# A one-core hybrid Hyena/S5 block: transfers issued earlier, x normalized in halves, the gate sums in 16 double steps, and one full-precision copy moved from VectorE to ScalarE

## The chip, the cores and the metric

One core of a Trainium2 chip, one launch of one program. The metric is device time in microseconds (us), first to last instruction of the core and what lies around it. TensorE (PE) multiplies, VectorE (DVE), ScalarE (ACT) and GpSimd (POOL) do the elementwise work, SyncE (SP) issues nearly all of the transfers, and each engine takes its instructions strictly in program order.

## The reference, cut to what matters

```
cond = silu(c), silu(c_ctx);  mod = cond @ w_ada + b_ada          # six parts of 1024: shift, scale, gate, twice
pc = (rms_norm(ctx) * g * (1 + scale_c) + shift_c) @ w_in         # 256 context tokens, S5 channels only
ctx_state = final S5 states of pc                                 # both directions
px = (rms_norm(x) * g * (1 + scale_x) + shift_x) @ w_in           # 1024 tokens: 1536 Hyena channels, 512 S5
yh = x0 * (fft_long_conv(x1 * v, filter) + bias * x1 * v)         # x0, x1, v: px after a 3-tap convolution
ys = gelu(S5 scan of px, started from ctx_state, both directions)
ys = ys * sigmoid(ys @ w_glu + b_glu)
x  = x + mod[2] * rms_norm(concat(yh, ys) @ w_out)
hx = modulated_norm(x, mod[3], mod[4])
x  = x + mod[5] * rms_norm(ConvGLU(hx))                           # w_up, 3x3 depthwise convolution, w_down
```

Everything is float32.

## The kernel before

A float32 matrix product is done as three matmuls on rounded operands: every operand is a rounded "high" tile (fp32r, made by ACT with a copy) and a "low" tile (what is left after subtraction of the high one, made by DVE or POOL), and lines 228, 229 and 230 issue high x high, low x high and high x low. So each piece of data passes through ACT and then DVE (or POOL) before PE can take it. Helpers record the engines' work, so one line stands for many places: line 143 is a two-tensor operation (`tt`), 146 a tensor-scalar one (`ts`), 149 a fused one (`stt`), 152 a load or store on SP's queue (`ld`), 161 an activation (`act`).

A scheduler decides the order of each engine's list from the program order and estimated due times. POOL's list is kept as written throughout, those of DVE and ACT from line 641 to 828, and SP's from line 1031 on. PE's list is always reordered. Buffers come from pools, so a transfer into a reused buffer waits until the last reader of its former content is done.

The stages, by the profile's clock: 
- 0 to 51 us, the front. Blocks of `w_ada` (512 KB each) are multiplied with the two condition vectors (line 308), giving shift and scale. x comes in as four tiles of 128 x 2 x 1024; for each, `sums_sq` (ACT, Square with a row sum into PSUM) gives the squares. `norm(c, n)` makes n columns of 1/rms (ACT square root, a few DVE operations of 128 x 8), and `apply` scales x (DVE, two operations of 128 x 1024 per tile). The modulation row is turned by four transposes (line 592), x by line 648, in eight column blocks, and `x_cols` (ACT from PSUM, with scale and shift per partition, then a DVE subtraction) makes the high and low operands.
- 51 to 120 us, the first projection (`x_mm`, eight steps), with the filter's work beside it. Ahead of the loop stands a scaling by -1 of `Cc[1]`, a table loaded as `k_c`.
- 120 to 205 us, the context: `ctx_cols` transposes a column block of ctx into PSUM (line 717), then makes c2's high part (ACT, Identity with scale and shift, rounded), the full value cv (DVE, tensor-scalar, from the same PSUM), and the low part (DVE, cv minus high).
- 205 to 405 us, four groups of Hyena channels, eight S5 batches' matmuls, and between them `gate_sums`: 32 steps, eight for each of mod parts 3, 4, 2 and 5. A step loads a block of `w_ada`, 1024 x 128, as one transfer of 512 KB into the ring `wm` of one buffer (`macc` takes the copied result), multiplies (line 691, 16 matmuls of 128 columns with 32 rows of output: eight matmuls, each of two passes), copies the 128 x 128 result to `acc` (ACT), sums its four row groups with a matmul against `sel` (line 693), adds the bias (ACT, Identity) and loads the next block. `sums_next(i)` takes a step; `MS` and `M_WIN` say how many steps stand at which places of the S5 loop.
- 405 to 585 us, the rest of S5 and of the Hyena spectra (`u_spec`, `product`, `inverse`; the latter on PE is line 1078), and the GLU gate of S5: `glu_w` (load a half of w_glu, split it), `glu_y` (split the S5 output), `glu_high`, `glu_low` (lines 1187, 1195) and in `glu_low` the sigmoid (ACT, into a single buffer `sg`) and the product ysT[n] * sg (DVE, 128 x 1024).
- 585 to 1445 us, w_out, the ConvGLU up and down, and the output.

Of the kernel before, what the change touches and what calls it, by code (L numbers as in the profile page):

```python
# [108 lines left out]
def hybrid_block(ctx: ExitStack, tc: tile.TileContext, t, out):  # L109
# [19 lines left out]
    def FRing(n, *dims, at=None):  # L129
        return Ring(sa, n, *dims, at=at)  # L130
# [541 lines left out]
    def gate_sums(gates, wm, acc, b0):  # L672
# [4 lines left out]
        def load(n):  # L677
            if n < len(steps):
# [7 lines left out]
        for n, (i, h) in enumerate(steps):  # L686
            w = ws_.pop(n)
            w3_ = w.rearrange("p (k c) -> p k c", k=8)
            for k in range(8):
                j = k % 4  # L690
                PE.matmul(PS[32 * j:32 * j + 32, b0[0], 0:128], lhsT=cond[:, k], rhs=w3_[:, k], start=k < 4, stop=k >= 4)  # L691
# [22 lines left out]
    def ctx_cols(k):  # L714
# [6 lines left out]
        ts(V, cv.rearrange("p j c -> p c j"), q, A0[:, k, 1:2], B0[:, k, 1:2], MUL, ADD)  # L721
# [35 lines left out]
    sums = gate_sums((3, 4, 2, 5), wm, macc, gb)  # L757
# [39 lines left out]
    for k in range(8):  # L797
# [366 lines left out]
    graw, sg = F(2, 512, at=(7,)), F(1024, at=(7,))  # L1164
    xin = FRing(2, 1024, at=(7,))
# [416 lines left out]
```

## Time and profile before

| | us |
|---|---|
| median of 3 runs (range) | 1447.63 (1445.07 to 1448.21) |
| the profiled execution | 1447.4 |
| its span, first to last instruction | 1445.6 |
| PE busy | 1326.1 (92%) |
| DVE busy | 883.5 (61%) |
| ACT busy | 482.3 (33%) |
| POOL busy | 472.5 (33%) |
| mean granted TensorE clock | 0.951 |

The execution is that of the profile, 1.8 us more than its span. "Busy" counts overlapping work per engine; PEld, the loading of weights into PE, runs beside the matmuls. An engine's average says little here, since the stages differ: each one is read by itself in the rows below. In a timeline row the first number is the start (us from the span's start), the second the time until the group's end, `xN` the count of instructions in it, and the bracket the idle time ahead of it with what ended it.

### The profile page before, as it was taken

How to read it: one execution, taken by the hardware profiler on the slowest of the kernel's cores; microseconds unless marked ns; L12 is line 12 of the kernel's file. 1: busy time of each engine (PE TensorE's matmuls, PEld its weight loads, DVE VectorE, ACT ScalarE, POOL GpSimd, SP SyncE). 2: the span in 40 equal slices, each digit the busy share in tenths (PEclk: the TensorE clock that was granted, in tenths of full speed). 3: DMA queues.
4: the chain of work that ended last, by engine and by line, in shares of the span. 5: the costliest groups of instructions: out<-in, count | busy, mean ns of one | idle time of the engine just before them, and what ended most of it. 6: DMA issues, size and time to landing. Idle time of an engine off the chain costs nothing.

```text
span 1445.6 us, 16905 instructions
## 1 busy us (share of the span) xinstructions
PE 1326.1 (92%) x6668; PEld 1071.5 (74%) x6668; DVE 883.5 (61%) x1208; ACT 482.3 (33%) x802; POOL 472.5 (33%) x250
## 2 busy tenths in 40 slices
PE   4888789899989957899999999999999999999997
PEld 0666567677767855787778888888888888888886
DVE  7776842456677999647766755755756757115314
ACT  3632122444433413346633222222222233224321
POOL 0000726556589203210122222222222226443540
PEclk8799899989998887999999999999999999999999
DMA  9423143545533225213311111111111115335422
GB/s 376 143 96 102 66 94 93 163 138 154 156 94 109 74 83 209 73 58 114 124 44 44 49 54 44 46 57 44 45 57 44 44 58 171 107 101 176 132 73 88
DMA packets 149639, 144.48 MB, mean 100 GB/s; under 512 B 29860, under 2 KB 128696, under 8 KB 147128
## 3 DMA queue, kind: packets, MB, share of 16 engines
q1 hardware_dynamic: 135000, 124.67, 27.9%
q10 hardware_dynamic: 14560, 18.74, 3.7%
q8 instruction: 52, 0.85, 0.2%
q14 instruction: 27, 0.22, 0.1%
HBM read 123.98 MB, written 19.37 MB: 99 GB/s over the span
## 4 chain that ended last, share of the span: by engine, by line
PE 73%; DVE 16%; DMA 5%; ACT 3%; issue 2%; SPq 1%; ACTq 0%; DVEq 0%
PE PS L228 21%; PE PS L229 21%; PE PS L230 21%; DVE s L143 12%; ACT s L161 3%; DMA s<-in_w_ada_dram 2%; DVE s L149 1%; PE PS L691 1%; PE PS L972 1%; DVE s L1001 1%; PE PS L428 1%; DMA s<-in_x_dram 1%; PE PS L936 1%; PE PS L429 1%; PE PS L1078 1%
## 5 line engine op out<-in xcount | busy, mean ns | idle before, releaser
L228 PE MATMUL PS<-s,s 128*128 128x512 f32 x1320 | 527.6, 401 | 4.2 <-ACT s L161 3.9
L229 PE MATMUL PS<-s,s 128*128 128x512 f32 x1320 | 524.1, 397 | 0.0
L230 PE MATMUL PS<-s,s 128*128 128x512 f32 x1320 | 523.1, 397 | 0.1
L161 ACT ACTIVATE s<-s 128x512 fp32r<-128x512 f32 (+9 forms) x356 | 259.6, 748 | 641.0 <-PE PS L229 208.2
L143 POOL TENSOR_TENSOR s<-s,s 128x1024 fp32r<-128x1024 f32 x98 | 252.2, 2577 | 613.5 <-ACT s L161 593.5
L143 DVE TENSOR_TENSOR s<-s,s 128x512 fp32r<-128x512 f32 (+6 forms) x178 | 196.8, 1117 | 218.7 <-ACT s L161 210.4
L143 POOL TENSOR_TENSOR s<-s 128x512 f32<-128x512 f32 (+2 forms) x147 | 219.0, 1503 | 262.4 <-PE PS L445 145.7
L228 PEld LDWEIGHTS PS<-s,s 128*128 128x128 f32 x1320 | 258.2, 196 | 59.9 <-ACT s L161 6.4
L230 PEld LDWEIGHTS PS<-s,s 128*128 128x128 f32 x1320 | 258.0, 196 | 53.8 <-issue 2.7
L229 PEld LDWEIGHTS PS<-s,s 128*128 128x128 f32 x1320 | 258.8, 196 | 52.5 <-issue 2.6
L149 DVE SCALAR_TENSOR_TENSOR s<-s,s 128x1024 f32<-128x1024 f32 x140 | 218.0, 1557 | 102.5 <-ACT s L161 98.3
L143 DVE TENSOR_TENSOR s<-s 128x512 f32<-128x512 f32 (+11 forms) x403 | 187.0, 500 | 41.9 <-DMA s<-s 27.1
L161 ACT ACTIVATE s<-PS 128x512 f32<-128x512 f32 (+6 forms) x212 | 110.8, 538 | 227.1 <-PE PS L429 53.2
L149 DVE SCALAR_TENSOR_TENSOR s<-s 128x1024 f32<-128x1024 f32 (+5 forms) x136 | 107.6, 807 | 54.9 <-ACT s L161 52.5
L161 ACT ACTIVATE s<-PS,s 128x128 f32<-128x128 f32 (+5 forms) x161 | 101.9, 680 | 81.7 <-PE PS L230 18.5
L143 DVE TENSOR_TENSOR s<-PS,s 128x512 f32<-128x512 f32 (+3 forms) x81 | 52.4, 668 | 62.5 <-ACT s L161 24.4
L230 PE MATMUL PS<-s 128*128 128x512 f32 x136 | 53.7, 395 | 0.0
L228 PE MATMUL PS<-s 128*128 128x512 f32 x136 | 53.4, 395 | 0.0
L229 PE MATMUL PS<-s 128*128 128x512 f32 x136 | 53.4, 392 | 0.0
L149 DVE SCALAR_TENSOR_TENSOR s<-PS,s,s 128x1023 f32<-128x1023 f32 x24 | 30.6, 1278 | 26.4 <-ACT s L161 25.9
L1078 PE MATMUL PS<-s,s 128*128 128x256 f32 x128 | 31.2, 406 | 15.6 <-DMA s<-in_k_idft_dram 14.8
L1078 PEld LDWEIGHTS PS<-s,s 128*128 128x128 f32 x128 | 26.1, 205 | 20.2 <-DVE s L143 16.1
(89 smaller groups left out, 803.0 us busy)
## 6 DMA issues: line engine op xcount, KB each, us to landing
s<-in_ffn_w_up_dram SPq DMA_DIRECT2D x44, 512.0 KB
s<-in_ffn_w_down_dram SPq DMA_DIRECT2D x44, 512.0 KB
s<-in_w_ada_dram SPq DMA_DIRECT2D x32, 512.0 KB
s<-in_w_in_dram SPq DMA_DIRECT2D x20, 512.0 KB
s<-in_w_ada_dram SPq DMA_DIRECT2D x8, 1024.0 KB
s<-in_x_dram SPq DMA_DIRECT2D x4, 1024.0 KB
kf_d<-s ACTq DMA_DIRECT2D x4, 1024.0 KB
s<-kf_d SPq DMA_DIRECT2D x4, 1024.0 KB
```

Source lines behind the costliest of these rows:

```text
L143: return pin(e, e.tensor_tensor(o, a, b, op=op))
L149: return pin(e, e.scalar_tensor_tensor(o, a, s, b, op0=op0, op1=op1))
L161: return pin(A, A.activation(o, i, f, **k))
L228: PE.matmul(dst, lhsT=hi, rhs=mh, start=first, stop=False)
L229: PE.matmul(dst, lhsT=hi, rhs=ml, start=False, stop=False)
L230: PE.matmul(dst, lhsT=lo, rhs=mh, start=False, stop=last)
L428: PE.matmul(o, lhsT=dft[:, c, r], rhs=hkb[:, r, 0], start=True, stop=False)
L429: PE.matmul(o, lhsT=dft[:, 2 * c, r2], rhs=hkb[:, r2, 1], start=False, stop=True)
L691: PE.matmul(PS[32 * j:32 * j + 32, b0[0], 0:128], lhsT=cond[:, k], rhs=w3_[:, k], start=k < 4, stop=k >= 4)
L936: PE.matmul(pk_[:, g], lhsT=d["G"][:, z, g * 128:(g + 1) * 128], rhs=CC[z][:, g].rearrange("p d q -> p (d q)"), start=z == 0, stop=z == 1)
L972: PE.matmul(PS[h:h + 64, bk, i * 160:(i + 1) * 160], lhsT=d["GT"][:, z, g * 128 + h:g * 128 + h + 64], rhs=u, start=True, stop=True)
L1078: PE.matmul(bk[:, 256 * j:256 * j + 256], lhsT=zb[:, k, c], rhs=idft[:, 2 * h + j, i], start=i == 0, stop=i == 3)
```

## The change

Four parts.

1. The front. `norm` and `apply` run for each half of x (four columns of row sums, two tiles) as soon as that half's squares are there, rather than once for all eight columns at the end. The scaling of `Cc[1]` moves from ahead of the projection loop to its step k = 3.
2. The context. The full value cv is made by ACT from PSUM with a second Identity activation, behind the rounded one; the DVE tensor-scalar goes. The rest of `ctx_cols` is unchanged.
3. The gate sums. 32 single steps become 16 double ones: a step multiplies two blocks (m = 0, 1) into 256 columns of PSUM, copies 128 x 256 at once, and issues the loads of the next two blocks. Each block comes as two transfers of 256 KB into four tiles (two halves of `wm`, two tiles of `w2_`). The summing matmuls and the bias (now a DVE two-tensor operation on 128 x 2) of a step stand at the head of the next one (`finish`). `gate_end`'s row goes through its own tile `grow_`. The sums are created behind `s5_load(0)`; `MS` goes from (1, 2, 2, 1, 1) to (1, 1, 1, 0, 1), and `sums_next(M_WIN)` leaves the context loop (M_WIN is 0).
4. The GLU gate. The raw w_glu has two buffers of its own at the top of a segment, and its two loads, `kf_load(3)`, `wo_load(4)`, `wo_load(5)` and the inverse DFT table in two halves are issued ahead of the load of ys4; before, ys4 came first, then the table, the two halves of w_glu in turn through one buffer, the w_out blocks, and the spectrum.

```diff
@@ the loop over w_ada blocks, and what follows it
-    norm(2, 8)
-    for q in range(4):
-        apply(V, xr[q], 2 + 2 * q)
+            if (k - SQ0) % 2:
+                h = k - SQ0 - 1
+                norm(2 + 2 * h, 4)
+                for q in (h, h + 1):
+                    apply(V, xr[q], 2 + 2 * q)
@@ gate_sums
-                ld(ws_[n].rearrange("p (k c) -> p k c", k=8),
-                   w_ada[:, c0:c0 + 128].rearrange("(k p) c -> p k c", p=128))
+                for u in range(2):
+                    ld(ws_[n][u].rearrange("p (k c) -> p k c", k=4),
+                       w_ada[512 * u:512 * u + 512, c0:c0 + 128].rearrange("(k p) c -> p k c", p=128))
...
-            act(acc, PS[:, b0[0], 0:128], AF.Copy)
-            PE.matmul(PS[:, b0[0], 128:130], lhsT=acc, rhs=sel, start=True, stop=True)
+        load(1)
+        def finish(n):
+            i, h = steps[n]
+            for m in range(2):
+                PE.matmul(PS[:, b0[0], 256 + 2 * m:258 + 2 * m], lhsT=acc[:, 128 * m:128 * m + 128], rhs=sel, start=True, stop=True)
...
-            act(SB2[:, z, h:h + 1], PS[:, b0[0], 128:129], AF.Identity, bias=bias[:, h:h + 1])
-            if h == 7:
+            tt(V, SB2[:, z, h:h + 2], PS[:, b0[0], 256:260:2], bias[:, h:h + 2], ADD)
+            if h == 6:
                 gate_end(i, b0[0])
-            load(n + 1)
+        for n in range(0, len(steps), 2):
+            if n:
+                finish(n - 2)
...
+            act(acc, PS[:, b0[0], 0:256], AF.Copy)
+            load(n + 2)
+            load(n + 3)
             yield
+        finish(len(steps) - 2)
@@ ctx_cols
-        ts(V, cv.rearrange("p j c -> p c j"), q, A0[:, k, 1:2], B0[:, k, 1:2], MUL, ADD)
+        act(cv.rearrange("p j c -> p c j"), q, AF.Identity, scale=A0[:, k, 1:2], bias=B0[:, k, 1:2])
@@ the projection loop
-    act(Cc[1], Cc[1], AF.Copy, scale=-1.0)
...
+        if k == 3:
+            act(Cc[1], Cc[1], AF.Copy, scale=-1.0)
@@ behind s5_load(0)
+    w2_ = [F(512, at=(2,)), F(512, at=(8,))]
+    macc, grow_ = F(256, at=(2, 8)), F(128, at=(0, 2, 8))
+    wmv = Views([[wm.b[0][:, 0:512], wm.b[0][:, 512:1024]], w2_])
+    sums = gate_sums((3, 4, 2, 5), wmv, macc, gb)
@@ the GLU gate
-    graw, sg = F(2, 512, at=(7,)), F(1024, at=(7,))
+    graw, sg = [T(2, 512) for _ in range(2)], F(1024, at=(7,))
...
+    for h in range(2):
+        ld(graw[h], t["s5_w_glu"][0, 256 * h:256 * h + 256].rearrange("(k p) c -> p k c", p=128))
+    kf_load(3)
+    wo_load(4)
+    wo_load(5)
+    for h in range(2):
+        ld(idft[:, 2 * h:2 * h + 2], t["k_idft"][:, 2 * h:2 * h + 2])
     ld(ys4, ys_d.rearrange("k p c -> p k c"))
-    ld(idft, t["k_idft"])
     glu_w(0)
     glu_w(1)
-    wo_load(4)
-    wo_load(5)
-    kf_load(3)
@@ constants
-MS, UF = (1, 2, 2, 1, 1), 1
+MS, UF = (1, 1, 1, 0, 1), 1
```

How the lists move, at three places. On PE at the front, before (s_0_69 is the modulation row, s_0_67 and s_0_68 the two halves of x, s_0_64 the identity, s_0_65 a filter table):

```order
L308 MATMUL PS<-s_0_69,s_0_64 32x512 x20
L592 MATMUL PS<-s_0_64,s_0_69 128x128 x4
L648 MATMUL PS<-s_0_64,s_0_67 128x128 x4
L648 MATMUL PS<-s_0_64,s_0_68 128x128 x4
L445 MATMUL PS<-s_0_65 128x512 x2
L648 MATMUL PS<-s_0_64,s_0_67 128x128 x4
L228 MATMUL PS<-s_1_300,s_1_301 128x512
```

and of the changed kernel:

```order
L308 MATMUL PS<-s_0_69,s_0_64 32x512 x20
L650 MATMUL PS<-s_0_64,s_0_68 128x128 x4
L594 MATMUL PS<-s_0_64,s_0_69 128x128 x4
L650 MATMUL PS<-s_0_64,s_0_67 128x128 x8
L228 MATMUL PS<-s_1_307,s_1_308 128x512
```

Lines 592 and 648 are 594 and 650 now. The transposes of one half of x stand ahead of those of the modulation row, and the filter's two matmuls (445) no longer stand between them and the first product.

On PE at the first gate steps, before (s_0_67 holds the block of w_ada in line 691's rows; 693 is the sum, 972 the S5 input product, 910 and 922 transposes of S5):

```order
L936 MATMUL PS<-s_0_65,s_0_68 128x32 x8
L229 MATMUL PS<-s_0_302,s_1_300 128x512
L691 MATMUL PS<-s_0_67,s_0_64 32x128 x8
L230 MATMUL PS<-s_1_301,s_1_300 128x512
L693 MATMUL PS<-s_0_64 128x2
L910 MATMUL PS<-s_0_64,s_0_67 128x128 x4
L972 MATMUL PS<-s_0_70 64x160 x4
L691 MATMUL PS<-s_0_67,s_0_64 32x128 x8
L972 MATMUL PS<-s_0_70 64x160 x3
```

and of the changed kernel, from the second block of step 0 on (line 706 is the former 691; s_0_68 and s_0_71 are the two tiles `w2_`):

```order
L706 MATMUL PS<-s_0_68,s_0_64 32x128 x4
L706 MATMUL PS<-s_0_71,s_0_64 32x128 x4
L922 MATMUL PS<-s_0_64,s_0_67 128x128 x4
L693 MATMUL PS<-s_0_64,s_0_68 128x2 x2
L984 MATMUL PS<-s_0_70 64x160 x9
L706 MATMUL PS<-s_0_67,s_0_64 32x128 x8
L706 MATMUL PS<-s_0_68,s_0_64 32x128 x4
L706 MATMUL PS<-s_0_71,s_0_64 32x128 x4
L984 MATMUL PS<-s_0_70 64x160
```

A double step's 16 matmuls stand together, the sums of the step before ahead of them, and between one step's second block and the next step's first there are 15 other instructions here.

On DVE in the GLU stage, before (s_2_2942 and s_1_2941 hold spectra; `s_0_65<-s_0_65` of 128x1024 is the product of ysT and the sigmoid):

```order
L143 TENSOR_TENSOR s_1_2941<-s_1_2941 128x512
L143 TENSOR_TENSOR s_2_2942<-s_2_2942 128x256 x2
L143 TENSOR_TENSOR s_2_2942<-s_2_2942 128x2x128
L143 TENSOR_TENSOR s_0_67<-PS,s_0_67 128x2x2x128
L143 TENSOR_TENSOR s_2_2942<-s_2_2942 128x2x128
L143 TENSOR_TENSOR s_1_2941<-s_1_2941 128x512
L143 TENSOR_TENSOR s_2_2942<-s_2_2942 128x512 x2
L143 TENSOR_TENSOR s_2_2942<-s_2_2942 128x256 x2
L149 SCALAR_TENSOR_TENSOR s_2_2942<-s_2_2942 128x256 x4
L143 TENSOR_TENSOR s_2_2942<-s_2_2942,s_1_2941 128x1024 x4
L143 TENSOR_TENSOR s_2_2942<-s_2_2942 128x4x128 x4
L143 TENSOR_TENSOR s_0_65<-s_0_65 128x1024
```

and of the changed kernel (s_2_2949 and s_1_2948 now):

```order
L143 TENSOR_TENSOR s_2_2949<-s_2_2949 128x256 x2
L143 TENSOR_TENSOR s_2_2949<-s_2_2949 128x2x128 x2
L143 TENSOR_TENSOR s_2_2949<-s_2_2949 128x256 x2
L143 TENSOR_TENSOR s_2_2949<-s_2_2949 128x512
L149 SCALAR_TENSOR_TENSOR s_2_2949<-s_2_2949 128x256 x4
L143 TENSOR_TENSOR s_2_2949<-s_2_2949 128x512
L143 TENSOR_TENSOR s_2_2949<-s_2_2949,s_1_2948 128x1024 x4
L143 TENSOR_TENSOR s_2_2949<-s_2_2949 128x4x128 x4
L143 TENSOR_TENSOR s_0_65<-s_0_65 128x1024
L143 TENSOR_TENSOR s_2_2949<-s_2_2949 128x512 x2
L143 TENSOR_TENSOR s_1_2948<-s_1_2948 128x4x256
L143 TENSOR_TENSOR s_0_65<-s_0_65 128x1024
```

The operations on s_1 (a spectrum's inverse, six in all, of which two stand in the rows of before and four shortly ahead of them) and two of 128x512 now follow the first product with the sigmoid instead of standing ahead of it.

## Rows read from the trace of the kernel before

**Rows 1.** Windows: busy us of PE, PEld, DVE, ACT, POOL; clock; DMA share; GB/s.

```profile
120.00:205.00 85.00, 64.86 (x300) 52.98 (x299) 59.05 (x108) 17.56 (x29) 28.60 (x23) 0.88 0.23 71
205.00:405.00 200.00, 188.96 (x1400) 141.07 (x1399) 94.77 (x92) 78.92 (x173) 122.77 (x87) 0.94 0.52 142
285.00:305.00 20.00, 17.02 (x121) 12.65 (x123) 14.46 (x14) 7.69 (x18) 9.38 (x8) 0.66 0.59 174
405.00:585.00 180.00, 137.74 (x841) 120.07 (x840) 164.94 (x181) 60.09 (x101) 80.80 (x42) 0.85 0.32 109
605.00:1300.00 695.00, 690.67 (x3059) 569.14 (x3058) 410.78 (x410) 219.24 (x322) 181.38 (x71) 1.00 0.23 69
```

**Rows 2.** Timeline of ACT, 0 to 52 us.

```profile
38.95 1.28 ACT L161 ACT_TABLE_LOAD   x1
...
47.60 1.57 ACT L161 ACTIVATE s<-s 128x512 f32<-128x512 f32 x2 [5.90 <-DMA s<-in_k_c_dram]
```

**Rows 3.** Timeline of DVE, 0 to 52 us.

```profile
30.22 4.07 DVE L143 TENSOR_TENSOR s<-s 128x512 f32<-128x512 f32 x6
...
41.53 5.39 DVE L146 TENSOR_SCALAR s<-s,s 128x1024 f32<-128x1024 f32 x8
```

**Rows 4.** Timeline of PE, 0 to 52 us.

```profile
41.75 1.12 PE L592 MATMUL PS<-s,s 128*128 128x128 f32 x4 [0.72 <-ACT s L161]
...
51.23 0.62 PE L228 MATMUL PS<-s,s 128*128 128x512 f32 x1
```

**Rows 5.** Groups by line and shape, 120 to 225 us: busy us, mean ns.

```profile
L161 ACT ACTIVATE s<-PS,s 128x256 fp32r<-128x256 f32 x8 | 6.5, 815 | 8.5 <-PE PS L717 8.5
...
L146 DVE TENSOR_SCALAR s<-PS,s 128x256 f32<-128x256 f32 x8 | 5.7, 716 | 0.9 <-ACT s L161 0.9
```

**Rows 6.** Timeline of DVE, 105 to 205 us.

```profile
156.00 12.45 DVE L143 TENSOR_TENSOR s<-s 128x512 f32<-128x512 f32 x8
```

**Rows 7.** Source view of line 691: what PE waited for (us, times).

```profile
  DMA s<-in_w_ada_dram: 8.2, 12
```

**Rows 8.** Chain of waits: two landings of a gate block.

```profile
270.85 4.98 DMA s<-in_w_ada_dram
...
321.84 4.25 DMA s<-in_w_ada_dram
```

**Rows 9.** Timeline of PE, 205 to 440 us: the matmuls of one gate block.

```profile
285.97 0.65 PE L691 MATMUL PS<-s,s 128*32 128x128 f32 x16
```

**Rows 10.** Timeline of SP's queue, 530 to 620 us.

```profile
539.18 19.78 SPq L152 DMA_DIRECT2D s<-in_s_w_glu_dram  x2
```

**Rows 11.** Timeline of PE, 530 to 620 us.

```profile
550.76 9.85 PE L1078 MATMUL PS<-s,s 128*128 128x256 f32 x32 [14.85 <-DMA s<-in_k_idft_dram]
...
584.04 3.44 PE L1187 MATMUL PS<-s 128*128 128x512 f32 x8 [3.96 <-ACT s L161]
...
587.32 2.00 PE L1187 MATMUL PS<-s,s 128*128 128x512 f32 x8
...
613.46 0.58 PE L228 MATMUL PS<-s,s 128*128 128x512 f32 x1
```

**Rows 12.** Timeline of ACT, 530 to 620 us.

```profile
582.87 1.11 ACT L161 ACTIVATE s<-PS,s 128x1024 f32<-128x1024 f32 x1 [7.99 <-DVE s L143]
```

**Rows 13.** Timeline of DVE, 530 to 620 us.

```profile
547.04 4.63 DVE L143 TENSOR_TENSOR s<-s,s 128x1024 fp32r<-128x1024 f32 x4 [1.43 <-ACT s L161]
551.59 8.12 DVE L143 TENSOR_TENSOR s<-s 128x512 f32<-128x512 f32 x8
...
560.62 2.88 DVE L143 TENSOR_TENSOR s<-s 128x512 f32<-128x512 f32 x6
...
579.15 9.44 DVE L143 TENSOR_TENSOR s<-s 128x512 f32<-128x512 f32 x12
```

**Rows 14.** Timeline of POOL, 530 to 620 us.

```profile
553.11 5.45 POOL L143 TENSOR_TENSOR s<-s,s 128x1024 fp32r<-128x1024 f32 x1 [71.28 <-ACT s L161]
563.42 7.73 POOL L143 TENSOR_TENSOR s<-s,s 128x1024 fp32r<-128x1024 f32 x3 [4.87 <-ACT s L161]
```

More of the change, by code (lines that the diff above doesn't have):

```diff
@@ L127, in R, with FRing @@
         return sa.get(*dims, dt=F32R, at=at)
-    def FRing(n, *dims, at=None):
-        return Ring(sa, n, *dims, at=at)
+    def FRing(n, *dims, **kw):
+        return Ring(sa, n, *dims, **kw)
     def RRing(n, *dims, at=None):
@@ L665, in gate_end @@
             tt(V, SB2[:, z], SB2[:, z], g13[:, z - 2], MUL)
-            PE.transpose(PS[:8, b0, 0:128], SB2[:, z], ident)
-            act(macc[:8], PS[:8, b0, 0:128], AF.Copy)
-            ld(g_d[z - 2][0].rearrange("(k c) -> k c", k=8), macc[:8])
+            PE.transpose(PS[:8, b0, 384:512], SB2[:, z], ident)
+            act(grow_[:8], PS[:8, b0, 384:512], AF.Copy)
+            ld(g_d[z - 2][0].rearrange("(k c) -> k c", k=8), grow_[:8])
     B2 = SB2[:, 0]
@@ L681, in load @@
                 c0 = i * 1024 + 128 * h
-                ld(ws_[n].rearrange("p (k c) -> p k c", k=8),
-                   w_ada[:, c0:c0 + 128].rearrange("(k p) c -> p k c", p=128))
+                for u in range(2):
+                    ld(ws_[n][u].rearrange("p (k c) -> p k c", k=4),
+                       w_ada[512 * u:512 * u + 512, c0:c0 + 128].rearrange("(k p) c -> p k c", p=128))
         load(0)
[L686 to L691, printed above, removed]
-            act(acc, PS[:, b0[0], 0:128], AF.Copy)
-            PE.matmul(PS[:, b0[0], 128:130], lhsT=acc, rhs=sel, start=True, stop=True)
+        load(1)
[3 more added lines that the diff above has]
+                PE.matmul(PS[:, b0[0], 256 + 2 * m:258 + 2 * m], lhsT=acc[:, 128 * m:128 * m + 128], rhs=sel, start=True, stop=True)
             z, bias = {3: (0, b34[:, 0:8]), 4: (1, b34[:, 8:16]), 2: (2, b25[:, 0:8]), 5: (3, b25[:, 8:16])}[i]
-            act(SB2[:, z, h:h + 1], PS[:, b0[0], 128:129], AF.Identity, bias=bias[:, h:h + 1])
-            if h == 7:
+            tt(V, SB2[:, z, h:h + 2], PS[:, b0[0], 256:260:2], bias[:, h:h + 2], ADD)
+            if h == 6:
                 gate_end(i, b0[0])
-            load(n + 1)
+        for n in range(0, len(steps), 2):
+            if n:
+                finish(n - 2)
+            for m in range(2):
+                w3_ = [w.rearrange("p (k c) -> p k c", k=4) for w in ws_.pop(n + m)]
+                for k in range(8):
+                    j = k % 4
+                    PE.matmul(PS[32 * j:32 * j + 32, b0[0], 128 * m:128 * m + 128], lhsT=cond[:, k], rhs=w3_[k // 4][:, j],
+                              start=k < 4, stop=k >= 4)
+            act(acc, PS[:, b0[0], 0:256], AF.Copy)
+            load(n + 2)
+            load(n + 3)
             yield
+        finish(len(steps) - 2)
+        yield
     g_d = [drp.tile([1, 1024], F32, name=f"g{i}_d") for i in range(2)]
-    macc = F(128, at=(0,))
     gb = [3]
@@ L756, in hybrid_block @@
     ld(ctx_t, ctx_d.rearrange("(i p) c -> p i c", p=128))
-    sums = gate_sums((3, 4, 2, 5), wm, macc, gb)
     sums_sq(ctx_t, 0, vj)
@@ L1091, in hybrid_block @@
             wm.put()
-            sa.put(macc)
+            sa.put(macc, grow_, *w2_)
             yh2 = F(2, 1024, at=(1,))
@@ L1230, in hybrid_block @@
                 f(n + m, 2 * m)
-    sa.put(graw, sg, yh, *yl, *gw)
+    sa.put(*graw, sg, yh, *yl, *gw)
     r_a = RRing(4, 2, 4, 128, at=(2,))
```

8 lines of the change are left out of this document (3 added, 5 removed).

## The prediction

> **What bounds the kernel.** I read the windows by stage first. From 605 to 1300 us PE is busy 690.67 of 695 us at full clock [rows 1], and the change touches nothing there: whatever is won or lost ahead of 605 us arrives at the end one for one. The question is therefore when the first w_out product starts, at 613.46 us [rows 11], and the stages ahead of it have different limits. At 120 to 205 us PE works 64.86 of 85, DVE 59.05, ACT 17.56: PE waits at times for the chain ACT, DVE, PE. At 205 to 405 PE works 188.96 of 200, so little is idle, but the granted clock is 0.94, and 0.66 at 285 to 305 (between the two levels, 1.2 and 2.4 GHz) [rows 1]. At 405 to 585 DVE works 164.94 of 180 and PE only 137.74 [rows 1]: there DVE's list is the path, and a PE wait alone is worth nothing. Second I read each engine's timeline at the seams of these stages, third the chain of waits for the gate blocks' landings. The profiled execution took 1447.4 us, 1.8 over its span and 0.2 under the median of the runs, so the sum is made from 1447.4.
>
> **The front.** Before, ACT finishes the last tile's squares at about 38.95, then loads the square root's table, 1.28 us [rows 2]; the eight scalings start at 41.53 and take 5.39, 0.674 each [rows 3], and end at 46.9. The transposes follow at once, but ACT's splitting of the first column block stands behind the scaling of `Cc[1]`, which sat idle 5.90 us for `k_c` and ends at 49.17 [rows 2]; the first product starts 2.06 us later, 51.23 [rows 4]. In the changed list the first half's norm comes behind DVE's six B operations, which end at 34.29 [rows 3]; its square root brings the table in ahead of the last squares. The second half's squares then end some 0.6 late (the first half's small operations are in ACT's and DVE's way; an estimate), there is no second table load, so the last scalings start at 41.53 - 1.28 + 0.6 = 40.85, and only four are left: 2.70 us, end 43.55. But the order on PE has the transposes of the second half ahead of those of the modulation row (1.12 us [rows 4]), and nothing goes on without that row: 43.55, some 0.65 for the last transpose, 1.12 and its small wait make 45.4, and copies and the first block's transposes 46.1. With the same 2.1 us from there to the product: 48.2, a gain of 3.0. The scaling moved to k = 3 costs ACT its 1.57 us behind the first product, when ACT is half idle: nothing. Bounds: 0, if the modulation row or w_in's split is what is late next, and 1.28 + 2.70 + 1.57 = 5.5, if all three go.
>
> **The context.** DVE loses eight operations of 716 ns, 5.7 us, and ACT gets eight more Identity activations of 815 ns, 6.5 us [rows 5]. ACT has room (17.56 of 85 [rows 1]), but the two activations of one block now follow each other, so the subtraction can start 0.815 later where DVE was already waiting for the block, and 0.716 earlier where DVE was late. DVE is late only in parts of the stage, above all from 156.00, where eight operations of 128 x 512 take 12.45 us [rows 6] (1.56 each, against 0.48 at 560.62 [rows 13]); I count a third of the stage. Gain: 5.7 / 3 = 1.9, less some latency elsewhere: 1.5. Bounds: a loss of 6.5 / 3 = 2.2, a gain of 4.
>
> **The gate sums.** Before, one buffer held the block, so a load could only start when the last matmul on it was done, and landed 4.25 to 4.98 us later [rows 8]. PE or its weight load stood 8.2 us in 12 waits for such landings [rows 7], besides waits for ACT's copies. Now a block's two tiles are free while the other block of the pair is multiplied. What PE has to do between the release of a tile and its next use at the tightest: the other block's 0.65 us [rows 9], and what the list has between a step and the next. At the first step these are 15 instructions, 30 in the trace's count, where each float32 product of line 691 shows as two; at the stage's mean of 188.96 / 1400 = 0.135 us [rows 1] 4.0, and as they are narrower than the mean I take 3.4: 4.1 us in all. By the same count six of the 15 steps are as tight, the others have 5 to 19 us. Taking the landing at 4.6, the middle of the two rows, the six tight steps wait 0.5 each, 3 us in place of 8.2: 5.2 gained. ACT loses 64 small operations and gets 16; DVE gets 16 of about 0.2 us, 3.2 us in a stretch in which it is busy 94.77 of 200 [rows 1]. But PE's next step cannot enter the PSUM bank until that DVE addition is done, and DVE is in order: behind it stand the scan's operations, and ahead of it what DVE was given before. I take this as hidden, since `finish` stands a whole step ahead of the next use. Part of the 0.66 clock at 285 to 305 came with these waits: 17.02 busy us at 0.66 would be 11.2 at full clock, so 5.8 at the most come back there; I take 0.8. The term is 6. Bounds: 8.2 + 5.8 = 14 gained, and a loss of 10, where pairs land late (second rival).
>
> The Trainium skill, DMA: Bandwidth & Descriptors, section Anatomy of one DMA, speaks against the halving: it gives each transfer a fixed cost of about 2.0 us whatever its size, and this page's section is on GpSimd's path, while the loads here go out on SP. By it, a half block would be 2.0 + (4.6 - 2.0) / 2 = 3.3 us as an estimate, and two in a row 6.6 instead of 4.6; whether they overlap no row of before shows, since it issues one at a time.
>
> **The GLU gate.** DVE, the path of this stretch, runs on without idle time ahead of its groups but for a wait of 1.43 at 547.04 [rows 13]. Before, the second sigmoid starts at 582.87 after 7.99 us of idle that ended with a DVE instruction [rows 12]: `sg` is one buffer, and the first product ysT * sg, which frees it, stands in DVE's list behind the inverse preparations of two spectra and product 3, inside the group at 579.15 [rows 13]. PE waits 3.96 for ACT at the same point [rows 11]. In the changed list this first product stands ahead of six operations on the spectrum of the inverse (two of 1024 and four of 512) and two more of 512: in columns of 512 that is ten. At 0.48 each (2.88 for six, 560.62) they are 4.8 us, and at 1.02 (8.12 for eight, 551.59) 10.2 [rows 13]; I take 5.5, near the lower, as POOL is idle when most of them run. The 1.43 wait for ACT goes, as w_glu is there earlier (it held SP's queue 19.78 us [rows 10]): half, 0.7, counts. The low products of output block 2 now partly stand ahead of the high ones of block 3: seven matmuls at 0.25 (2.00 for eight [rows 11]) fill 1.7 of the 3.96. Together 5.5 + 0.7 + 1.7 = 7.9, taken as 8: the first w_out product some 8 us nearer to the front's and the gate's gains. The wait for the inverse table, 14.85 [rows 11], shortens by itself, but it lies beside a full DVE and is not counted.
>
> Against this stands POOL. Its four subtractions, 5.45 and 7.73 us [rows 14], come earlier, beside DVE's product 2. Where POOL runs, DVE's operations of 128 x 512 took 1.02 (551.59) instead of 0.48 (560.62) [rows 13], and they will do so wherever the four fall: moved, not removed.
>
> The Trainium skill, SBUF — State Buffer, section Who interferes with whom, says a DVE operation with two SBUF inputs contends with a GpSimd instruction that reads SBUF, over a shared port pair that whoever starts first holds. The 1.02 against 0.48 agrees with it. By that rule the move under product 2 would take as much from DVE there as it gives back later, so no gain comes from POOL's shift alone; I have counted none.
>
> Bounds for this stage: 2, where only the small items are real, and 13, with the list at the higher rate.
>
> **Sum.** 1447.4 - 3.0 - 1.5 - 6 - 8 = 1428.9, so 1429.
>
> **Rivals.**
> A. The transfers are not earlier than before. The order of issue is not the time of issue: the two table halves and w_glu wait for buffers of the last S5 batch, and if these come free at about 538 us, where SP issued before, the gate comes as late; likewise a gate pair that lands as late as single blocks did. For it: the w_glu issue stood 19.78 us on SP [rows 10] because of a buffer. Against it: w_glu has its own tiles now. Then the GLU stage gives 2 and the gate sums 2: 1447.4 - 3 - 1.5 - 2 - 2 = 1438.9.
> B. More comes back. The clock rises in the gate stretch (5.8) and the list gives the higher rate (13): 1447.4 - 3 - 1.5 - 11 - 13 = 1418.9, and with the front at its bound about 1415.
> C. Slower: the pairs. If the transfers of a pair go one behind the other, a pair needs 2 x 4.6 = 9.2 us, and the six tight steps wait 9.2 - 4.1 = 5.1 each, 30.6 for 8.2 before: a loss of 22.4, less the other three terms' 12.5: +9.9, 1457. It decides from 4.1 + (8.2 + 12.5) / 6 = 7.5 us per pair. For it: 512 KB took 4.25 to 4.98 us alone [rows 8]; DMA share is 0.59 at 285 to 305 [rows 1], so the queues aren't empty. Against it: 0.59 leaves room, and 174 GB/s there is little.
>
> **How the numbers follow.** The forecast holds 0.60, its own range 1421 to 1436 (front 0 to 5.5, gate 2 to 10, end 4 to 11, not all on one side). A holds 0.18, B 0.10, C 0.09, and 0.03 goes to no change. The range of 8 in 10 runs from B's lower part to A's upper: 1414 to 1443. 0.2% is 2.9 us, about what a measurement of this kernel can tell from no change: faster (under 1444.7) holds the forecast, B and nearly all of A, 0.86; within, 0.05; slower, C, 0.09.
>
> **What would show it.** In the changed profile: one table load before 36 us and none at 39, and the first product at about 48.2; ACT at 24 and DVE at 53 busy us in the former 120 to 205; PE's waits for w_ada under 4 us in six places, and the clock at 0.9 or more in the stretch of 285 to 305; the second sigmoid some 7 us nearer to the last S5 batch; the first w_out product near 595 us. Wrong: waits for w_ada of 3 us and more at each pair (C), SP issuing w_glu at 530 or later or the sigmoid's idle still near 8 (A), a subtraction in the context that waits for ACT at every block.

## The result and the profile after

The changed kernel takes 1426.06 us in the median of four runs (1424.16 to 1428.53), the kernel before 1447.92 in four (1445.07 to 1452.89): a ratio of 0.9832, 95% interval 0.9807 to 0.9856, 1.7% faster. Run again beside the last experiments it gave 0.9815 (0.9792 to 0.9838). The forecast was 1429 us. The sum agreed better than any of its terms: two were too large and two too small, and that they cancelled in part is luck. Of the other signs, ACT's and DVE's busy time in the former 120 to 205 us are 22.66 and 55.01 (24 and 53 forecast), and the first w_out product starts at 596.12 (595).

The windows of the changed kernel, same stretches as [rows 1]:

```profile
120.00:205.00 85.00, 66.64 (x316) 54.44 (x316) 55.01 (x104) 22.66 (x38) 31.05 (x26) 0.90 0.29 83
205.00:405.00 200.00, 189.72 (x1455) 147.13 (x1454) 115.49 (x114) 71.29 (x130) 138.41 (x90) 0.95 0.52 144
285.00:305.00 20.00, 18.07 (x137) 13.19 (x133) 16.45 (x15) 9.96 (x19) 13.57 (x9) 0.76 0.46 132
405.00:585.00 180.00, 146.76 (x840) 127.33 (x839) 159.19 (x179) 66.43 (x105) 81.86 (x41) 0.86 0.33 110
605.00:1300.00 695.00, 690.71 (x3064) 568.87 (x3063) 414.26 (x431) 223.42 (x335) 179.06 (x70) 1.00 0.23 70
```

From 205 to 405 us PE is as full as before (189.72 against 188.96), but DVE has done 115.49 us of work in place of 94.77, some 20 us more.

For the comparison of kernels I cut each profiled execution at five marks: the first projection product (line 228), the two stores of the S5 inputs (`us_d`, the ends of the projection loop and of the context loop), the last stores of the S5 outputs (`ys_d`, of which each S5 batch has four), and the first w_out product. Each mark is the start of its instruction. Three of the marks in the kernel before and in the changed one, timelines of ACT (before, then after):

```profile
121.46 0.62 ACTq L762 DMA_DIRECT2D us_d<-s  x1
...
202.80 0.53 ACTq L814 DMA_DIRECT2D us_d<-s  x1
```

```profile
121.78 0.62 ACTq L775 DMA_DIRECT2D us_d<-s  x1
...
198.09 0.53 ACTq L826 DMA_DIRECT2D us_d<-s  x1
...
520.49 2.77 ACTq L1040 DMA_DIRECT2D ys_d<-s  x4
```

Before, the last `ys_d` stores began at 533.84, the first w_out product at 613.46. The length of each stage, in us, of one profiled execution per kernel (parts in the order of the change; the labels are explained with the experiments):

| kernel | front | projection | context | S5 and gates | GLU | rest |
|---|---|---|---|---|---|---|
| before | 51.2 | 70.2 | 81.3 | 331.0 | 79.6 | 832.1 |
| changed | 48.0 | 73.8 | 76.3 | 322.4 | 75.6 | 830.6 |
| changed, again | 46.9 | 72.9 | 76.4 | 318.9 | 75.4 | 830.5 |
| part 1 alone | 46.9 | 72.8 | 81.4 | 338.4 | 78.4 | 832.4 |
| part 2 alone | 51.2 | 69.8 | 77.7 | 334.2 | 81.5 | 832.1 |
| part 3 alone | 50.4 | 70.5 | 82.9 | 321.9 | 80.2 | 830.7 |
| part 4 alone | 50.0 | 70.4 | 82.9 | 336.2 | 75.3 | 830.6 |
| eight single steps a batch | 51.4 | 70.4 | 82.5 | 350.9 | 81.3 | 830.9 |
| part 3, last steps late | 52.0 | 70.2 | 82.9 | 315.8 | 81.5 | 831.8 |
| changed, bias on ACT | 46.2 | 72.6 | 76.3 | 331.4 | 76.1 | 830.7 |
| changed, four POOL operations out | 46.7 | 72.6 | 77.5 | 319.5 | 68.8 | 831.6 |
| changed, without part 1 | 50.2 | 70.1 | 76.1 | 324.3 | 76.2 | 830.6 |
| changed, the four on DVE | 49.3 | 72.8 | 76.3 | 321.6 | 68.8 | 831.6 |
| the same, without part 1 | 51.3 | 70.4 | 76.3 | 319.0 | 68.7 | 830.6 |

Within a column the kernels fall into two groups, by whether they have the part that acts there, and the groups do not overlap, but for the S5 column of the changed kernel with the bias on ACT, which is as long as those with single steps. The spread inside a group, up to 8.5 us in the S5 column, is that of single executions.

### The profile page after: what moved, and what is told of

It reads as the page before. It is cut to its first block, busy times and chain, and to the rows that moved or that the text cites. A ratio compares the mean times of both kernels' runs of the same rounds, so it can differ in the third digit from the quotient of the medians.

```text
span 1426.7 us, 16933 instructions
## 1 busy us (share of the span) xinstructions
PE 1317.9 (92%) x6668; PEld 1071.9 (75%) x6668; DVE 885.9 (62%) x1222; ACT 476.6 (33%) x763; POOL 482.2 (34%) x250
## 4 chain that ended last, share of the span: by engine, by line
PE 73%; DVE 14%; DMA 5%; ACT 3%; issue 2%; POOL 2%; ACTq 0%; SPq 0%; DVEq 0%; POOLq 0%
PE PS L228 21%; PE PS L229 21%; PE PS L230 21%; DVE s L143 11%; ACT s L161 3%; POOL s L143 2%; DVE s L149 2%; DMA s<-in_w_ada_dram 1%; DMA s<-in_x_dram 1%; PE PS L1094 1%; PE PS L706 1%; DVE s L1013 1%; PE PS L1202 1%; PE PS L428 1%; PE PS L429 1%
## 5 line engine op out<-in xcount | busy, mean ns | idle before, releaser
L161 ACT ACTIVATE s<-s 128x1024 fp32r<-128x1024 f32 (+10 forms) x357 | 259.8, 746 | 664.8 <-PE PS L229 214.3
L143 DVE TENSOR_TENSOR s<-s,s 128x512 fp32r<-128x512 f32 (+6 forms) x178 | 200.3, 1135 | 188.4 <-ACT s L161 180.2
L143 POOL TENSOR_TENSOR s<-s 128x512 f32<-128x512 f32 (+2 forms) x147 | 225.5, 1548 | 244.8 <-DVE s L143 171.1
L228 PEld LDWEIGHTS PS<-s,s 128*128 128x128 f32 x1320 | 257.7, 196 | 58.9 <-ACT s L161 5.2
L229 PEld LDWEIGHTS PS<-s,s 128*128 128x128 f32 x1320 | 258.7, 196 | 54.0 <-issue 3.4
L230 PEld LDWEIGHTS PS<-s,s 128*128 128x128 f32 x1320 | 258.0, 196 | 53.1 <-issue 1.8
L143 DVE TENSOR_TENSOR s<-s 128x512 f32<-128x512 f32 (+11 forms) x406 | 191.6, 505 | 28.8 <-DMA s<-s 21.2
L161 ACT ACTIVATE s<-PS 128x512 f32<-128x512 f32 (+5 forms) x196 | 107.1, 567 | 199.6 <-PE PS L429 50.4
L161 ACT ACTIVATE s<-PS,s 128x128 f32<-128x128 f32 (+5 forms) x137 | 98.5, 783 | 68.3 <-PE PS L230 18.6
L143 DVE TENSOR_TENSOR s<-PS,s 128x512 f32<-128x512 f32 (+4 forms) x97 | 54.9, 583 | 98.0 <-PE PS L693 32.4
L143 DVE TENSOR_TENSOR s<-s,PS 128x1024 f32<-128x1024 f32 x21 | 25.6, 1221 | 23.7 <-ACT s L161 23.7
```

Source lines behind the costliest of these rows:

```text
L143: return pin(e, e.tensor_tensor(o, a, b, op=op))
L161: return pin(A, A.activation(o, i, f, **k))
L228: PE.matmul(dst, lhsT=hi, rhs=mh, start=first, stop=False)
L229: PE.matmul(dst, lhsT=hi, rhs=ml, start=False, stop=False)
L230: PE.matmul(dst, lhsT=lo, rhs=mh, start=False, stop=last)
```

## The experiments

Five rounds each; the ratio is to the kernel before on the same chip, with its 95% interval.

**The four parts alone.** Each is the kernel before with one part of the diff shown above and nothing else.

Part 1. 

> The kernel before with part 1 alone (x in halves, the scaling of Cc[1] at k = 3). The prediction's front term: -3.0 us, carried to the end, 1444.5. Rival, from the trace of the changed kernel: the first product comes 3.3 us earlier, but the two filter matmuls that stood in the idle time ahead of it now stand behind it (1.9 us) and the clock is at its lower level for as long as before (44 to 52 us instead of 47 to 52), so the context's first transposes (121.6 us before) come where they came and the time is within 1 us of before.

Measured: 1.0012 (0.9999 to 1.0025). The front is 4.3 us shorter and the projection 2.6 longer; the first `us_d` store comes at 119.77 (121.46 before). The rival was right in the main: most of the gain is gone behind the projection, and none reaches the end.

Part 2. 

> The kernel before with part 2 alone (the full value of the context block by ACT). The prediction's term: -1.5 us, with DVE late for a third of the stage. Rival: DVE's list is the path in the whole stage, so nearly all of the 5.7 us that leave it are gained: the last transposes of the stage (198.10 us before) come 4.5 to 5 us earlier, and the time is 4 to 5 us under before.

Measured: 0.9976 (0.9962 to 0.9991), 3.5 us, between 1.3 and 5.5. The context stage takes 77.7 us, 3.6 less, and its last transposes come 4.0 us earlier (194.13). That is nearer to the rival than to the predicted term, but the interval of the time holds both.

Part 3. 

> The kernel before with part 3 alone (16 double gate steps). The prediction's term: -6 us, most of it in the stage itself by fewer waits for w_ada (8.2 us before, under 3 now). Rival: the waits for w_ada go, but PE now waits up to 15 us for DVE's addition of the bias, so the stage itself gives under 2 us at the fourth S5 batch's output (413.05 us before); what the part gives comes later, because the gate steps end some 30 us earlier and S5's batches follow sooner: -5 to -9 us in all by the last batch's output (533.84 before).

Measured: 0.9903 (0.9884 to 0.9921), 14 to 15 us, more than twice the predicted term and more than the rival's. The stage of S5 and the gates takes 321.9 us. As the rival said, the fourth batch's output hardly moves (411.42; 413.05 before) and the gain is there at the last (525.70; 533.84).

Part 4. 

> The kernel before with part 4 alone (w_glu in two buffers, loads of the GLU stage issued earlier). The prediction's term: -8 us between the last batch's output and the first w_out product (79.6 us before). Rival: the second sigmoid comes 8 us earlier, but the inverse's DVE operations that were put behind the first product are late next, slowed to 2 us each beside POOL's subtractions, and PE waits 4 to 5 us for them: the stretch gets 4 us shorter and the time falls by 4 to 5 us.

Measured: 0.9972 (0.9959 to 0.9984), 4.1 to 4.5 us; the stretch is 75.3 us. The rival was right.

The four ratios multiply to 0.986, the changed kernel has 0.983; the intervals do not tell the two apart.

**Eight single steps a batch.** Is it the earlier end of the gate steps that pays?

```diff
-MS, UF = (1, 2, 2, 1, 1), 1
+MS, UF = (2, 2, 2, 1, 1), 1
```

> The kernel before with MS = (2, 2, 2, 1, 1): the 32 single gate steps stand eight to a batch in place of seven, so that the last falls into the fourth batch and no longer ahead of the fifth batch's products; buffers, transfers and steps are those of before. Theory 1 (what part 3 gives is the earlier end of the gate steps: DVE's scans of the fifth batch start about 15 us earlier, 404 in place of 419.6): 7 to 12 us faster than before, although the waits for w_ada grow from 8.2 to 12 or more. Theory 2 (the gain is that of the double step's fewer waits): 0 to 3 us slower than before.

Measured: 1.0102 (1.0082 to 1.0122), 15 us slower, worse than either theory. The waits of PE and its weight loads for w_ada grow to 14.0 us in 18, and those of DVE for ACT from 45.2 + 29.3 us to 61.4 + 31.4 (205 to 405 us). By the clock the gate steps did not end earlier, though: the last sum starts at 408.87, and at 407.85 before. The fifth batch's scans start at 435.32, 16 us later than before and not 15 earlier. So this run does not test an earlier end.

**Part 3 with its last steps late.** The converse: the double steps, with the last ones at later places of the list, where the last single steps stood.

```diff
-        msl = MS if n < 5 else (0,) * 5
+        msl = (0, 0, 1, 0, 1) if n == 0 else MS if n < 5 else (0,) * 5
```

> Part 3 alone, with two double steps fewer in the first batch, so that the last two double steps and their sums stand in the fifth batch at the places at which the last single steps stood before. Theory 1 (the gain is the earlier end): at least half of the 14 us that part 3 alone gave goes, the time is 0 to 7 us under before, and the fifth batch's scans start at 412 us or later. Theory 2 (fewer waits): 10 us or more under before, as for part 3 alone.

Measured: 0.9891 (0.9872 to 0.9909), as for part 3 alone. The first scan of the fifth batch on DVE, in part 3 alone, with the last steps late, and with eight single steps a batch (419.57 in the kernel before):

```profile
404.11 1.48 DVE L1010 TENSOR_TENSOR_SCAN s<-s,s 128x640 f32<-128x640 f32 x1
```

```profile
402.23 1.48 DVE L1010 TENSOR_TENSOR_SCAN s<-s,s 128x640 f32<-128x640 f32 x1
```

```profile
435.32 4.64 DVE L1001 TENSOR_TENSOR_SCAN s<-s,s 128x640 f32<-128x640 f32 x2
```

The experiment was to bring the scans later than in part 3 alone, and they came 2 us earlier. What did come later is the last gate sum, 391.70 in place of 381.89, and these 10 us cost nothing. That the earlier end is not what pays is shown for these 10 us alone; the last sum is still 16 us earlier than before. What in the double step pays, neither run says; the next one does in part.

**The bias on ACT again.**

```diff
-            tt(V, SB2[:, z, h:h + 2], PS[:, b0[0], 256:260:2], bias[:, h:h + 2], ADD)
+            for m in range(2):
+                act(SB2[:, z, h + m:h + m + 1], PS[:, b0[0], 256 + 2 * m:257 + 2 * m], AF.Identity, bias=bias[:, h + m:h + m + 1])
```

> The changed kernel with the bias of the gate sums added by ACT again (two Identity activations of 128 x 1 a double step) in place of DVE's addition. In the changed kernel PE and its weight loads stood 15.0 us in 8 waits for that addition, and DVE 32.4 us in 8 waits for the sums' matmuls. Theory 1: these waits are on the path of the S5 batches: 3 to 8 us under the changed kernel. Theory 2: PE's work comes a little earlier but the batches are bound by their own chain through ACT, POOL and DVE: within 2 us of the changed kernel (0.983 of before).

Measured: 0.9887 (0.9865 to 0.9910): against 0.9832 of the changed kernel 8 us slower. Both theories were wrong, in the other direction from theory 1: 32 operations of some 0.26 us on ACT, with the waits that they bring, cost more than DVE's 16 additions. What PE and its weight load waited for at the gate's matmuls, the source view of their line, first the changed kernel, then this one (us, times):

```profile
  DVE s L143: 15.0, 8
  issue: 6.6, 18
  DMA s<-in_w_ada_dram: 2.8, 8
```

```profile
  ACT s L161: 25.8, 11
  issue: 5.4, 13
  DMA s<-in_w_ada_dram: 4.4, 5
```

The wait for DVE's 15.0 does not vanish, it becomes one for ACT of 25.8, 11 us more; the S5 stage loses 9 to 12.5 (331.4 against 322.4 and 318.9). With 331.4 the double steps are no shorter than single ones (331.0 to 338.4), but that is one profile; the times are firmer, and by them 8 us of part 3's 14 hang on who adds the bias, and not on halving the steps.

**Four POOL subtractions left out.**

```diff
-        split(wo[k], wo_raw[k], G)
+        if k in (6, 7, 0, 1):
+            act(wo[k][:, 0], wo_raw[k], AF.Copy)
+            act(wo[k][:, 1], wo_raw[k], AF.Copy, scale=0.0)
+        else:
+            split(wo[k], wo_raw[k], G)
```

> The changed kernel with the low parts of w_out's blocks 6, 7, 0 and 1 written as zeros by ACT, so four of POOL's subtractions of 128 x 1024 in the GLU stage are left out of the computation. Theory 1 (the six operations of the inverse that were deferred behind the first product are late next because they run beside POOL at 2.04 us for 128 x 1024): they fall to about 1.2 us each or less, PE's wait of 4.6 us ahead of the inverse goes, and the time is 3 to 5 us under the changed kernel. Theory 2 (the deferral alone makes them late): PE still waits 3 us or more there and the time is within 2 us of the changed kernel.

Measured: 0.9778 (0.9759 to 0.9797), 5 to 8 us under the changed kernel (0.9815 and 0.9832); the GLU stretch falls from 75.6 to 68.8. Theory 1 was right, and its price low: the stretch lost 6.8 us, not 3 to 5.

**The changed kernel again, without part 1, and with the four subtractions on DVE.** These four ran on one chip.

> The changed kernel itself, on the chip of the three runs that follow: 0.983 of before.

Measured: 0.9815 (0.9792 to 0.9838).

> The changed kernel with part 1 undone (x in one piece, Cc[1] scaled ahead of the projection loop). The prediction's front term: 3 us slower than the changed kernel. Rival (the projection loop gives the front's 3.3 us back, because DVE's and ACT's filter chain is the path from 60 to 120 us): within 1 us of the changed kernel at the context's first transposes (121.1 us) and at the end.

Measured: 0.9838 (0.9817 to 0.9858), 3 us over the changed kernel with intervals that overlap. The context's mark, though, comes at 120.29 here, and at 121.78 and 119.83 in the two profiles of the changed kernel: the difference arose behind the projection.

```diff
-        split(wo[k], wo_raw[k], G)
+        split(wo[k], wo_raw[k], V if k in (6, 7, 0, 1) else G)
...
-    for k in (6, 7):
-        wo_split(k, (6,))
-        wo_load(k - 6)
     inverse(1, 6)
     inverse(2, 6)
     inverse(3, 6)
+    for k in (6, 7):
+        wo_split(k, (6,))
+        wo_load(k - 6)
```

> The changed kernel with the four subtractions for w_out's blocks 6, 7, 0 and 1 made by DVE behind the inverse's operations, in place of POOL beside them. If it is POOL that slows the inverse's operations to 2.04 us for 128 x 1024, they fall to about 1.03, PE's wait of 4.6 us goes, and the four subtractions (1.2 us each, 4.9 in all) stand where DVE waits for PE: 4 to 7 us under the changed kernel. If the four on DVE are late for the w_out products: within 2 us of it.

Measured: 0.9775 (0.9754 to 0.9796), 1419.25 us in the median against 1424.25 of the changed kernel beside it. It is faster than the kernel before and, by 5 us, than the changed one.

> The kernel of the run before with part 1 undone as well. If part 1 costs 1 to 2 us as its run alone showed (1.0012 of before): 1 to 2 us under the run before. If it gives 3 us: 3 us over it.

Measured: 0.9773 (0.9751 to 0.9795), the same as the run before. So part 1 changed the time by +1.7, -3.3 and +0.3 us in three pairs: nothing that these runs can tell from zero.

## Why the prediction was right, and where its steps were not

**The front: the step was right, its carrying on was not.** The rows of the changed kernel that answer to [rows 2] and [rows 4], ACT first (the table load, the last square root), then PE:

```profile
29.10 1.28 ACT L161 ACT_TABLE_LOAD   x1
...
39.38 0.21 ACT L161 ACTIVATE s<-s 128x4 f32<-128x4 f32 x1 [0.24 <-DVE s L146]
```

```profile
43.70 1.06 PE L594 MATMUL PS<-s,s 128*128 128x128 f32 x4
...
47.97 0.78 PE L228 MATMUL PS<-s,s 128*128 128x512 f32 x1
...
57.17 1.88 PE L445 MATMUL PS<-s 128*128 128x512 f32 x4
```

One table load before 36 us, none at 39, and the first product at 47.97 (48.2 forecast). But the sum carried these 3 us to the end undiminished. From the first w_out product on, that held (the last column of the table, 830.5 to 832.4); from the front to there it failed at once. With part 1 the front is 46.2 to 49.3 us and the projection 72.6 to 73.8; without, 50.0 to 52.0 and 69.8 to 70.5. Summed, the end of the projection comes at 120.3 us on average in the six profiles with part 1 and at 121.2 in the eight without. One place where the gain goes shows in the PE timeline of the kernel before:

```profile
47.25 3.62 PE L445 MATMUL PS<-s 128*128 128x512 f32 x4
```

The filter's four matmuls filled the gap in front of the first product there; in the changed kernel they stand behind it, at 57.17, and take 1.88 us on the path. The first products also ran at the lower clock, 1.2 GHz: granted 0.50 from 48 to 52 us, 0.43 us from one to the next, and 0.23 to 0.25 from 52 us on. In this profile the filter's chain through ACT and DVE is as before within 0.4 us from 60 us on; the second profile of the changed kernel keeps 1.6 us of the gain (`us_d` at 119.83). Worth: about 1 us by the marks, where 3.0 was summed, inside the stated bounds of 0 to 5.5; by the times it is not told from zero.

**The context: the size was off.** Groups by line and shape of the changed kernel, which answer to [rows 5]: count, busy us, mean ns, idle before.

```profile
L161 ACT ACTIVATE s<-PS,s 128x256 fp32r<-128x256 f32 x8 | 6.5, 814 | 4.5 <-PE PS L730 4.5
L161 ACT ACTIVATE s<-PS,s 128x256 f32<-128x256 f32 x8 | 6.2, 778 | 0.0
```

The operation costs on ACT what was estimated. The step that failed is "I count a third of the stage": it asks when the subtraction can start, and not who else waits for the operation that leaves DVE. PE did, since the next block's transposes go into the PSUM that it reads. PE's waits from 120 to 205 us and the longest of them in PE's timeline, before:

```profile
PE PS L717 <- DVE s L146: 10.0, 3, 8.1
```

```profile
169.13 0.69 PE L717 MATMUL PS<-s,s 128*128 128x128 f32 x2 [8.10 <-DVE s L146]
```

The longest stood behind the eight operations at 156.00 of [rows 6]. In part 2 alone and in the changed kernel no transpose waits for DVE, though a part returns: the filter's matmuls (445) wait 12.5 and 11.9 us for DVE, 2.9 before. The stage shrinks by 3.6 us in part 2 alone, at a granted clock of 0.90 in both kernels, and by 5.7 on average, from 82.3 us in the six profiles without part 2 to 76.6 in the eight with it; there the granted clock is also higher (0.87 to 0.90 without, 0.90 to 0.93 with). So the term is worth some 3.5 to 5.7, and the bound of 4 may have been too narrow.

**The gate sums: right in the waits for w_ada, wrong in what they are worth.** The remaining waits are 2.8 us in 8 (3 forecast, 8.2 before [rows 7]). But the stage gave 14.5 us: 335.0 on average in the four profiles with single steps as before, 320.4 in the eight with double steps and the bias on DVE. The step that failed is "ACT loses 64 small operations and gets 16", which stands in the sum without a price, while all of the price was put on the w_ada landings. Waits of DVE from 205 to 405 us, the kernel before and the changed one (for whom, us in total, times, longest):

```profile
DVE s L143 <- ACT s L161: 45.2, 10, 10.6
DVE s L149 <- ACT s L161: 29.3, 3, 15.4
```

```profile
DVE s L143 <- PE PS L693: 32.4, 8, 8.4
DVE s L149 <- ACT s L161: 23.0, 2, 14.8
...
DVE s L143 <- ACT s L161: 10.0, 5, 3.1
```

DVE waited 74.5 us for ACT, now 33.0 (59.1 to 79.3 in the other three profiles with single steps as before). ACT's copy and bias of each gate step wait for PE, and ACT goes in order, so what S5 needs of ACT stood behind them. Who waited for the gate's matmuls, the last line of the source view, before and after:

```profile
  ACT s L161: 48.0, 27
```

```profile
  ACT s L161: 28.5, 11
```

DVE's new waits for the sums, 32.4 us, bring its total back to 65.4, but it is 20 us further by 405 us. The windows of part 3 alone, of part 3 with its last steps late, and of the changed kernel with the bias on ACT, 205 to 405 us, to be read at the third busy time, DVE's, against 94.77 in [rows 1]:

```profile
205.00:405.00 200.00, 189.25 (x1441) 146.09 (x1442) 114.30 (x117) 72.49 (x133) 138.68 (x90) 0.95 0.54 149
```

```profile
205.00:405.00 200.00, 185.99 (x1445) 144.81 (x1444) 121.80 (x123) 73.83 (x134) 138.85 (x90) 0.96 0.54 149
```

```profile
205.00:405.00 200.00, 183.02 (x1407) 142.21 (x1406) 110.50 (x94) 76.03 (x162) 131.71 (x86) 0.93 0.49 139
```

Eight single steps a batch left DVE at 84.31 and ended last. But DVE's progress alone does not set the stage's length: with the bias on ACT it is 16 us further than before, and the stage is as long. PE's wait for DVE's addition, which the prediction took as hidden, is not (15.0 us in 8), but it costs less than what it replaces.

The S5 and gate stage as a whole, windows of the kernel before and of the changed one:

```profile
202.80:533.84 331.04, 297.76 (x2123) 237.91 (x2122) 212.31 (x221) 127.25 (x262) 190.39 (x124) 0.91 0.42 120
```

```profile
198.09:520.49 322.40, 292.84 (x2122) 239.14 (x2122) 219.82 (x239) 117.08 (x214) 196.89 (x124) 0.92 0.46 136
```

PE does the same matmuls in less busy time: 299.7 us on average in the four profiles with single steps, at a granted clock of 0.90 to 0.92, and 289.7 in the eight with double steps and the bias on DVE, at 0.92 to 0.94. So some 10 of the 14.5 us go with a higher clock, and the rest is less idle time of PE. The prediction took 0.8 us for the clock, from the stretch of 285 to 305 us; that stretch is no measure of it, as two profiles of the changed kernel show 0.76 and 0.91 there, and the slower kernel with eight single steps a batch 0.81. What stays open: whether the clock rose because PE's work came with fewer gaps, and, as the scheduler wrote a different list for each of these kernels and no run held the list fixed, how much is fewer waits at ACT's head and how much a better interleaving of the batches.

**The GLU gate: the first half right, then a wait that took its place.** The second sigmoid, ACT's timeline of the changed kernel (before, [rows 12]):

```profile
561.13 1.12 ACT L161 ACTIVATE s<-PS,s 128x1024 f32<-128x1024 f32 x1 [3.93 <-DVE s L143]
```

It comes 40.6 us behind the last `ys_d` stores, 49.0 before: 8.4 nearer, where some 7 was forecast. The price of 0.48 us behind that is misread: the six operations at 560.62 of [rows 13] are three of 128 x 512 and three of 128 x 256, and alone these take 0.68 and 0.41. By shape, the two of 1024 (1.22) and six of 512 make 6.5 us, where 5.5 was taken; the 1.56 in the context mixes shapes too. Then half of the gain is lost. DVE, POOL and PE of the changed kernel:

```profile
536.02 4.52 DVE L143 TENSOR_TENSOR s<-s,s 128x1024 fp32r<-128x1024 f32 x2 [4.39 <-ACT s L161]
...
569.02 10.22 DVE L143 TENSOR_TENSOR s<-s 128x1024 f32<-128x1024 f32 x5 [1.03 <-ACT s L161]
```

```profile
567.99 5.69 POOL L143 TENSOR_TENSOR s<-s,s 128x1024 fp32r<-128x1024 f32 x2 [25.21 <-ACT s L161]
575.08 3.09 POOL L143 TENSOR_TENSOR s<-s,s 128x1024 fp32r<-128x1024 f32 x1 [1.40 <-ACT s L161]
```

```profile
580.30 16.17 PE L1094 MATMUL PS<-s,s 128*128 128x256 f32 x64 [4.61 <-DVE s L143]
596.12 0.58 PE L228 MATMUL PS<-s,s 128*128 128x512 f32 x1
```

The five at 569.02 are the products with the third and fourth sigmoid and three operations of the inverse. They run beside POOL's subtractions for the next w_out blocks, and PE waits 4.61 for what stands behind them. The step that failed is "as POOL is idle when most of them run": it held for what follows directly on the first product, up to 568 us, and not for what that pushed back. The 1.43 wait of DVE for ACT did not shrink either, it is 4.39. With the four on DVE behind the inverse, DVE, POOL and PE:

```profile
568.63 4.70 DVE L143 TENSOR_TENSOR s<-s 128x1024 f32<-128x1024 f32 x5 [1.18 <-ACT s L161]
```

```profile
527.86 14.37 POOL L143 TENSOR_TENSOR s<-s,s 128x1024 fp32r<-128x1024 f32 x4 [57.62 <-ACT s L161]
591.22 4.78 POOL L143 TENSOR_TENSOR s<-s,s 128x1024 fp32r<-128x1024 f32 x2 [48.99 <-ACT s L161]
```

```profile
569.10 20.02 PE L1094 MATMUL PS<-s,s 128*128 128x256 f32 x92
588.77 0.58 PE L228 MATMUL PS<-s,s 128*128 128x512 f32 x1
```

The same five operations by shape (busy us, mean ns), in the changed kernel (569.00 to 579.17 us) and with the four on DVE (568.60 to 573.25):

```profile
L143 DVE TENSOR_TENSOR s<-s 128x1024 f32<-128x1024 f32 x3 | 6.9, 2336 | 1.0 <-ACT s L161 1.0
L143 DVE TENSOR_TENSOR s<-s 128x512 f32<-128x512 f32 x2 | 3.4, 1759 | 0.0
```

```profile
L143 DVE TENSOR_TENSOR s<-s 128x1024 f32<-128x1024 f32 x3 | 3.6, 1222 | 1.2 <-ACT s L161 1.2
L143 DVE TENSOR_TENSOR s<-s 128x512 f32<-128x512 f32 x2 | 1.3, 685 | 0.0
```

They take 4.70 us in place of 10.22, PE does not wait, and the stretch is 6.8 us shorter. This agrees with the rule of the Trainium skill, SBUF — State Buffer, section Who interferes with whom: operations of DVE with two SBUF inputs contend with GpSimd's reads. The prediction used it for the four subtractions of w_glu and of blocks 4 and 5, found no gain, and did not ask what the deferred operations would meet.

**The rivals.** A did not occur: ACT split w_glu from 523.36 us on, 11.6 us ahead of the S5 output's blocks. C did not either: PE's waits for w_ada fell. Of B, the clock did rise in the gate stretch and came with most of what the gate sums gave beyond their term; the higher rate of the list, its other half, did not come. 1.0, 5.7, 14.5 and 4.7 (the GLU stretch, 80.4 on average in the six profiles without part 4 and 75.7 in the five with it and POOL's four) make 25.9 us, against the 18.5 of the sum and the 22 to 27 that the runs show. The terms were off by 2.0 and 3.3 us too much and 4.2 and 8.5 too little, so the time was right by mechanisms of which only the waits for w_ada, the earlier sigmoid and the earlier first product came as written. (B's lower end, the front at its bound, is 1416.4 by its own numbers, not 1415.)

## What to carry to other kernels

A gain at a seam is worth what the next stage's limit leaves of it: follow the path through the stage behind before carrying it on. When an operation leaves an engine, ask who waits for it, also for the buffer that it reads. A small instruction that waits for another engine costs, on an in-order engine, what is queued behind it: here it paid to put the bias on DVE, which had idle time, and not on ACT. Before a gain is put down to fewer waits, compare the busy time of PE and its granted clock. When operations are moved, ask what runs on the neighbouring engines at the new place; two-input work of DVE beside POOL took twice its time here, and moving four subtractions behind it shortened the stretch by 6.8 us, the whole fourth part of the change by 4.7. And read the price of an operation by its shape: a row of a timeline can mix several.

## What the runs showed of the hardware

A transfer of 256 KB, issued on SP's queue as one of a row of four, was on the chain of waits with 4.12 and 5.12 us from its own issue in the two profiles of the changed kernel and 4.20 to 5.84 in part 3 with its last steps late. One of 512 KB took 4.25 to 4.98 alone [rows 8]. So no half block that shows landed in the 3.3 us that the prediction estimated, and those with three others in flight landed in little more than the time of one. DVE's two-tensor operation on two SBUF operands took 1.22 us for 128 x 1024 and 0.69 for 128 x 512 (685 ns) with POOL idle, and 2.34 and 1.76 on average beside POOL's subtractions.
